# Storing the convolution branch as two halves, loading a merge's groups ahead, and transposing before scoring

## The chip, the cores and the metric

The kernel runs on one core of a Trainium2 chip. The metric is the device time of one execution in microseconds (us). Five engines matter: PE multiplies matrices, ACT (ScalarE), DVE (VectorE) and POOL (GpSimd) work elementwise, and SP issues nearly all DMA transfers. Each of them takes its instructions in the order in which the program lists them, and waits for other engines on semaphores.

## The reference

One layer for 1024 prompt tokens and 32 sample tokens, so T = 1056 columns, all in float32. Cut to what matters here:

```python
h, b_gate, c_gate, q, k, v, g_conv, g_att = split(xn @ w_in)
u = c_gate * h
y_conv = conv_w[0]*u[t-2] + conv_w[1]*u[t-1] + conv_w[2]*u[t]     # causal, 3 taps
conv_out = (b_gate * y_conv) @ w_conv_out
# for each of three dilation groups, 8 heads: softmax(q k / 8 + bias) v, with its log-sum-exp
wts = softmax(stack(lses), axis=0); o = sum(wts * stack(outs), axis=0)
attn_out = o @ w_attn_out
x = x + gate1 * ((sigmoid(g_conv) * conv_out + sigmoid(g_att) * attn_out) @ w_o)
x = x + gate2 * (relu(norm(x) @ w_mlp_in)**2 @ w_mlp_out)
```

## The kernel before

Activations lie with 128 features on the partitions and the 1056 columns along them. Every float32 operand of a large product is split in two: `hi`, a copy rounded to the matmul type fp32r, and `lo`, the remainder `x - hi`; three matmuls (hi·hi, hi·lo, lo·hi) make one product. A tile of 352 columns and 1024 features takes 24 matmuls (L377).

The program is written out by hand in one order. Long matmul jobs set the beat: after each half tile (or each bank of a paired job) `slot()` is called, and it emits other work in between: first what `later` holds for this slot (a list of functions with a countdown in slots), then attention work (`bg`, as far as a credit of `rate` per slot allows), then two paced lanes (`paced[0]`: the sample tokens' attention, `paced[1]`: the merges), whose generators say with `yield n` how many slots they pause.

The stages, with the times of the trace before:

- **Paired jobs** (about 130 to 430 us). Jobs H, C and B for two feature blocks at a time (`pair_job`, seven products n = 0 to 6, each for two column halves p = 0, 1, so 14 slots a job). Each product's bank is emptied by ACT or DVE: ACT copies n = 0 to `ps_s` (L269) and n = 2 to `ps_z` (L274). The p = 1 half uses one of two PSUM banks called `ps_s`, so the matmuls of n = 2, p = 1 can begin only when n = 0, p = 1 has been copied out. POOL forms sums of weights (`ws`, L229 to L232) and multiplies y, a page `yc` of 128x1056, by the gate in job B (L839); y is then stored to `yb_d` in DRAM (L846) during the next job. There are four such rounds, a store of two pages each.
- **Projections q, k, v with the prompt's attention between them** (about 540 to 1140 us). A visit of `attention` takes a pair of tiles: P·V of the pair before last, scores of this pair (L973, DVE adds the bias and takes the maximum in L979, ACT takes the exponent in L987), and transposes (L102) of the pair before, whose results DVE or ACT copy from banks `ps_pt` and `ps_g` to `S` (L99, L96). The decode lane and the sample values use the one bank `ps_pt` too.
- **Convolution output** (about 1140 to 1280 us): three chunks of 352 columns, eight tiles each. `conv_ops` loads the eight pages of a chunk from `yb_d` (`ybr`, L672) and splits them (`ybh` on ACT, `ybl` on DVE or POOL) in steps placed by `later`. The last attention visits, the decode lane's last group and merges run beside it.
- **Merges** (`merge`, one for each of four head pairs): weights of the three groups to DRAM (`w_d`), then for each group a broadcast load of its weights (`wb`, two DMAs) and its output (`og`), a product on DVE (L1252), a sum on POOL (L1257); at the end a split to `oh` and `ol` (L1263, L1265). All four must be done before the **attention output** (24 tiles of 12 matmuls, from about 1282 us), which reads them.
- Then w_o, and the channel mixer.

Of the kernel before, what the change touches and what calls it, by code (L numbers as in the profile page):

```python
# [9 lines left out]
F32 = mybir.dt.float32  # L10
F32R = mybir.dt.float32r
AF = mybir.ActivationFunctionType
ALU = mybir.AluOpType
# [9 lines left out]
KD = 8  # L23
# [26 lines left out]
class Trunk:  # L50
# [613 lines left out]

    def conv_ops(self, ch):
        nc = self.nc
        out, raws = [], {}

        def load(i):
            raw = raws[i] = self.page("ybr", (P, 3, CH))  # L670
            for x in range(3 if i < 2 else 2):
                nc.sync.dma_start(out=raw[:, x], in_=self.yb_d[3 * i + x][:, ch * CH:(ch + 1) * CH])  # L672

        def work(i):
            raw = raws.pop(i)
            h, l = self.page("ybh", (P, 3, CH), F32R), self.page("ybl", (P, 3, CH), F32R)
            for x in range(3 if i < 2 else 2):
                self.split(h[:, x], l[:, x], raw[:, x], CH, lo_on="pool" if x % 2 else "dve")
                out.append((h[:, x], l[:, x]))
            if i < 2:  # L680
                load(i + 1)
                self.later.append((2, lambda: work(i + 1)))
        load(0)
        self.later.append((2, lambda: work(0)))
        return out

    def qk_epilogue(self, is_k, g, j, c, ps, st):
# [138 lines left out]
    def conv_b(self, m):  # L826
        nc = self.nc

        def fin(mi, t, p, a, ps, op, last):
            if not last:  # L830
                b = self.chunk("ps_t")[:, :H]
            else:
                b = a
            c0 = (2 * p + t) * H
            nc.vector.tensor_tensor(out=b, in0=a, in1=ps, op=op)

            def mul():
                y = self.y[mi][:, c0:c0 + H]
                nc.gpsimd.tensor_tensor(out=y, in0=y, in1=b, op=ALU.mult)  # L839
            if last:  # L840
                mul()
            else:
                self.later.append((3, mul))

        def store(i):
            nc.sync.dma_start(out=self.yb_d[m + i], in_=self.y[i])  # L846
            self.y[i] = None
        for i in range(2):
            self.later.append((16 + i, lambda i=i: store(i)))
        return fin  # L850

    def keep_gate(self, i, g):
# [70 lines left out]
    def attention(self):  # L923
        st = {}
        p1 = p2 = None
        while True:
            pair = [self.items.popleft() for _ in range(2)] if self.items else None
            if pair is None and p1 is None and p2 is None:
                if self.done:
                    break  # L930
                yield None
                continue
            cost = 400
            if pair is not None and pair[0][2]:
                u = pair[0][0]
                if u["bias"] is None:
                    u["bias"] = self.load_bias(u["g"], u["j"])
                self.values(u)
                yield -1200
            for it in p2 or ():  # L940
                self.att_pv(it, st)
                cost += 120 * it[1][2]
            if pair is not None:
                self.att_scores(pair, st)
                cost += sum(450 + 130 * it[1][2] for it in pair)
            for it, n in zip(p1 or (), ("pt", "g")):
                self.att_tr(it, st, n)
                cost += 200 * it[1][2]
            yield -cost
            if p2 is not None and p2[1][3] and p2[1][0]["g"] == ORDER[2]:  # L950
                self.paced[1].append(self.merge(p2[1][0]["j"]))
            p1, p2 = pair, p1
# [270 lines left out]
    def merge(self, j):  # L1223
        nc = self.nc
        wk = self.chunk("wk", (P, 4, 2, 16))
        wk, M = wk[:, 0:3], wk[:, 3]
        for g in range(3):
            nc.sync.dma_start(out=M if g == 2 else wk[:, g], in_=self.st_d[g][j].rearrange("s h (b i) -> (h b) s i", i=16))
        yield 2
        nc.vector.tensor_copy(wk[:, 2].rearrange("p s (t y) -> p s t y", y=2), M.rearrange("p s (y t) -> p s t y", y=2))  # L1230
        mm, s = [wk[:, g, 0] for g in range(3)], [wk[:, g, 1] for g in range(3)]
        nc.vector.tensor_tensor(out=M[:, 0], in0=mm[0], in1=mm[1], op=ALU.max)
        nc.vector.tensor_tensor(out=M[:, 0], in0=M[:, 0], in1=mm[2], op=ALU.max)
        nc.vector.tensor_tensor(out=wk[:, :, 0], in0=wk[:, :, 0], in1=M[:, 0:1].to_broadcast([P, 3, 16]), op=ALU.subtract)
        nc.scalar.activation(wk[:, :, 0], wk[:, :, 0], AF.Exp)
        nc.vector.tensor_tensor(out=wk[:, :, 1], in0=wk[:, :, 0], in1=wk[:, :, 1], op=ALU.mult)
        nc.vector.tensor_tensor(out=M[:, 0], in0=s[0], in1=s[1], op=ALU.add)
        nc.vector.tensor_tensor(out=M[:, 0], in0=M[:, 0], in1=s[2], op=ALU.add)
        nc.vector.reciprocal(M[:, 1], M[:, 0])
        nc.vector.tensor_tensor(out=wk[:, :, 0], in0=wk[:, :, 0], in1=M[:, 1:2].to_broadcast([P, 3, 16]), op=ALU.mult)  # L1240
        yield 1
        nc.sync.dma_start(out=self.w_d[j].rearrange("g h (b i) -> (h b) g i", i=16), in_=wk[:, :, 0])
        del wk, M, mm, s
        yield 1
        acc = None
        for g in range(3):
            w, o = self.page("wb", (P, NP)), self.page("og", (P, NP))
            for hh in range(2):
                nc.sync.dma_start(out=w[64 * hh:64 * hh + 64], in_=self.w_d[j][g, hh].unsqueeze(0).to_broadcast([64, NP]))
            nc.sync.dma_start(out=o, in_=self.o_d[g][j])  # L1250
            yield 3
            nc.vector.tensor_tensor(out=o, in0=o, in1=w, op=ALU.mult)  # L1252
            del w
            if acc is None:
                acc = o
            else:
                nc.gpsimd.tensor_tensor(out=acc, in0=acc, in1=o, op=ALU.add)  # L1257
            del o
            yield 1
        yield 1  # L1260
        self.oh[j], self.ol[j] = self.page("oh", dt=F32R), self.page("ol", dt=F32R)
        yield 1
        nc.scalar.copy(self.oh[j][:, 0:NP], acc)  # L1263
        yield 1
        nc.vector.tensor_tensor(out=self.ol[j][:, 0:NP], in0=acc, in1=self.oh[j][:, 0:NP].bitcast(F32), op=ALU.subtract)  # L1265
        del acc
        yield 1
# [3 lines left out]
    def run(self):  # L1271
# [10 lines left out]
        self.o_d = [self.dp.tile([4, P, NP], F32, name=f"o_d{g}") for g in range(3)]  # L1282
        self.st_d = [self.dp.tile([4, 2, 2, NP], F32, name=f"st_d{g}") for g in range(3)]
        self.w_d = self.dp.tile([4, 3, 2, NP], F32, name="w_d")
        self.yb_d = self.dp.tile([KD, P, T], F32, name="yb_d")
        self.gate_d = self.dp.tile([16, P, T], F32, name="gate_d")

        w_in = t["w_in"]
# [53 lines left out]
        def begin(g, j, st):  # L1342
            self.sample_values(g, j, st["v"]["v"])
            self.add_unit(g, j, st["q"], st["k"], st["v"]["v"])
            if (g, j) == units[-1]:
                self.done = True
                self.rate = 1500.0
            else:
                self.rate = self.work / 18 * 0.85

# [607 lines left out]
```

## Time and profile before

| | |
|---|---|
| median of three executions | 2165.97 us (2165.32 to 2166.70) |
| the profiled execution | 2163.8 us, of which the traced span 2162.0 us |
| PE busy | 2021.7 us, 94% of the span |
| DVE, ACT, POOL busy | 65%, 46%, 36% |
| DMA | 325.84 MB, mean 151 GB/s |

Times in the rows are microseconds from the start of the span. A busy PE counts matmuls whose pipelined ends overlap. PEclk is the granted TensorE clock as a share of full speed.

### The profile page before, as it was taken

The numbers are of one execution on the slowest core, as the hardware profiler recorded it, in microseconds if no ns is written. First come the engines' busy times: TensorE is split into PE (matmuls) and PEld (weight loads), VectorE is DVE, ScalarE is ACT, GpSimd is POOL, SyncE is SP. The second block draws the span as 40 slices with busy tenths as digits, with TensorE's granted clock in tenths as the row PEclk, the third lists the DMA queues.
The fourth block names the chain that finished last, engine by engine and source line by source line (L and its number), as shares of the span: only waits on it lengthen the run. The fifth ranks groups of instructions, "written<-read, shape, count | busy, mean of one in ns | idle before, by whom it ended". The sixth has DMA issues, their size and how long they took to land.

```text
span 2162.0 us, 38832 instructions
## 1 busy us (share of the span) xinstructions
PE 2021.7 (94%) x15092; PEld 1907.2 (88%) x15092; DVE 1404.3 (65%) x2935; ACT 989.3 (46%) x2193; POOL 782.6 (36%) x553
## 2 busy tenths in 40 slices
PE   5899999999999999999997989988999999999998
PEld 2799999889899888888886878988999999999998
DVE  4846665435656666556676676378444447999997
ACT  4522223335566556555554322355555556433332
POOL 3645555320111111100011114235233235788785
PEclk8899999999999999999998999999999999999999
DMA  7242221764122445333246774432347729555542
GB/s 284 71 136 62 79 70 35 250 212 148 45 69 74 144 149 167 104 114 116 67 125 199 238 233 145 162 125 88 130 158 274 256 90 350 203 202 198 197 158 102
DMA packets 138096, 325.84 MB, mean 151 GB/s; under 512 B 34232, under 2 KB 77880, under 8 KB 136888
## 3 DMA queue, kind: packets, MB, share of 16 engines
q1 hardware_dynamic: 137480, 323.17, 44.5%
q8 instruction: 118, 1.93, 0.4%
q14 instruction: 66, 0.54, 0.1%
q10 hardware_dynamic: 432, 0.20, 0.0%
HBM read 270.48 MB, written 112.07 MB: 177 GB/s over the span
## 4 chain that ended last, share of the span: by engine, by line
PE 56%; DVE 23%; ACT 5%; issue 3%; DMA 3%; POOL 2%; SPq 0%; DVEq 0%; POOLq 0%; ACTq 0%
PE ps_g L377 23%; DVE acc L1721 5%; DVE wprod L162 5%; PE ps_g L264 4%; PE ps_s L264 4%; PE ps_g L266 4%; PE ps_s L266 4%; PE ps_s L265 4%; PE ps_g L265 4%; DVE hl L1573 1%; DVE wlo L197 1%; ACT S L987 1%; PE ps_o L1015 1%; DVE S L979 1%; PE ps_s L973 1%
## 5 line engine op out<-in xcount | busy, mean ns | idle before, releaser
L162 DVE TENSOR_TENSOR wprod<-wraw,wprod 128x512 fp32r<-128x512 f32 x276 | 270.1, 981 | 173.9 <-ACT wprod L158 173.8
L377 PE MATMUL ps_g<-xh,whi 128*128 128x352 f32 x1056 | 356.6, 338 | 12.8 <-ACT whi L193 6.5
L377 PE MATMUL ps_g<-xh,wlo 128*128 128x352 f32 x1056 | 346.3, 328 | 5.6 <-DVE wlo L197 5.4
L377 PE MATMUL ps_g<-xl,whi 128*128 128x352 f32 x1056 | 346.6, 328 | 3.0 <-POOL xl L406 2.2
L377 PEld LDWEIGHTS ps_g<-xh,whi 128*128 128x128 f32 x1056 | 203.2, 192 | 35.6 <-issue 16.1
L158 ACT CAST wprod<-wraw 128x512 fp32r<-128x512 f32 x276 | 163.3, 618 | 151.0 <-DVE wprod L162 104.1
L377 PEld LDWEIGHTS ps_g<-xl,whi 128*128 128x128 f32 x1056 | 203.9, 193 | 5.9 <-POOL xl L406 4.0
L377 PEld LDWEIGHTS ps_g<-xh,wlo 128*128 128x128 f32 x1056 | 202.7, 192 | 7.2 <-DVE wlo L197 7.2
L197 DVE TENSOR_TENSOR wlo<-wraw,whi 128x512 fp32r<-128x512 f32 x184 | 130.0, 748 | 45.6 <-PE ps_g L377 25.4
L162 POOL TENSOR_TENSOR lo<-qn,hi 128x1024 fp32r<-128x1024 f32 x12 | 33.2, 2770 | 346.7 <-ACT hi L158 346.7
L277 POOL TENSOR_TENSOR ps_z<-ps_z,ps_s 128x264 f32<-128x264 f32 x64 | 60.3, 944 | 252.0 <-DVE ps_s L276 251.8
L264 PE MATMUL ps_s<-th,wprod 128*128 128x264 f32 x512 | 146.3, 286 | 1.7 <-DVE ps_s L276 1.7
L264 PE MATMUL ps_g<-th,wprod 128*128 128x264 f32 x512 | 146.9, 287 | 0.0
L266 PE MATMUL ps_g<-th,wprod 128*128 128x264 f32 x512 | 145.8, 285 | 0.0
L265 PE MATMUL ps_s<-tl,wprod 128*128 128x264 f32 x512 | 145.8, 285 | 0.0
L266 PE MATMUL ps_s<-th,wprod 128*128 128x264 f32 x512 | 145.7, 285 | 0.0
L265 PE MATMUL ps_g<-tl,wprod 128*128 128x264 f32 x512 | 145.5, 284 | 0.0
L987 ACT ACTIVATE S<-S,ng 128x128 f32<-128x128 f32 (+1 forms) x192 | 84.2, 441 | 124.7 <-DVE ng L982 122.8
L193 ACT CAST whi<-wraw 128x512 fp32r<-128x512 f32 x184 | 104.2, 619 | 32.1 <-DMA wraw<-in_w_conv_out 11.4
L264 PE MATMUL ps_g<-xh,wprod 128*128 128x264 f32 x384 | 110.6, 288 | 3.2 <-ACT wprod L158 3.2
L266 PE MATMUL ps_g<-xh,wprod 128*128 128x264 f32 x384 | 110.3, 287 | 3.5 <-DVE wprod L162 3.5
L264 PE MATMUL ps_s<-xh,wprod 128*128 128x264 f32 x384 | 109.9, 286 | 3.4 <-DVE ps_s L280 3.4
(383 smaller groups left out, 6448.3 us busy)
## 6 DMA issues: line engine op xcount, KB each, us to landing
wraw<-in_w_in SPq DMA_DIRECT2D x76, 512.0 KB, 4.1
wada<-in_w_ada SPq DMA_DIRECT2D x48, 512.0 KB, 5.6
hid_d<-hid SPq DMA_DIRECT2D x32, 528.0 KB, 2.9
wraw<-in_w_mlp_in SPq DMA_DIRECT2D x32, 512.0 KB, 6.1
wraw<-in_w_mlp_out SPq DMA_DIRECT2D x32, 512.0 KB, 3.9
hraw<-hid_d SPq DMA_DIRECT2D x56, 264.0 KB, 4.4
kv<-in_v SPq DMA_DIRECT2D x28, 512.0 KB, 5.6
wraw<-in_w_conv_out SPq DMA_DIRECT2D x24, 512.0 KB, 6.7
```

What stands on the lines that cost most here:

```text
L158: nc.scalar.copy(hi, src)
L162: eng.tensor_tensor(out=lo, in0=src, in1=hi.bitcast(F32), op=ALU.subtract)
L193: self.nc.scalar.copy(hi[:, s], w[:, s])
L197: self.nc.vector.tensor_tensor(out=lo[:, s], in0=w[:, s], in1=hi[:, s].bitcast(F32), op=ALU.subtract)
L264: nc.tensor.matmul(ps, hi, xh, start=(k == 0), stop=False)
L265: nc.tensor.matmul(ps, hi, xl, start=False, stop=False)
L266: nc.tensor.matmul(ps, lo, xh, start=False, stop=(k == 3))
L277: nc.gpsimd.tensor_tensor(out=z[p], in0=z[p], in1=s[p], op=ALU.add)
L377: self.nc.tensor.matmul(ps, a, x, start=(i == 0), stop=(i == n - 1))
L973: nc.tensor.matmul(ps[hh][:, 256 * i:256 * i + N], q[a][pr, q0:q0 + P], k[b][pr, k0:k0 + N], start=(x == 0), stop=(x == 2))
L987: nc.scalar.activation(s, s, AF.Exp, bias=ng[:, hh, i:i + 1], accum_out=sm[:, hh, i:i + 1])
L1721: nc.vector.tensor_tensor(out=a, in0=a, in1=ps, op=ALU.add)
```

## The change

Three edits, and a number. (1) y is split where it is made: `later` places, for each of the two pages of a round, an ACT copy to a new page `yh` (`high`), a DVE subtraction in place (`low`), and two stores, to `ybh_d` and `ybl_d` (`store`). On SP's queue the two weight loads (L180) that stood behind the first store of a round stand ahead of all four. `conv_ops` only loads the halves, three pages a DMA. (2) `merge` has its loads in a function, and loads group g + 1 before it handles group g, with fewer pauses: 10 slots from the store of the weights to the copy `oh`, where there were 15. (3) In a visit the transposes come before the scores. The attention's `rate` behind the last unit is 2000 in place of 1500.

```diff
     def conv_ops(self, ch):
-        out, raws = [], {}
+        out = []
         def load(i):
-            raw = raws[i] = self.page("ybr", (P, 3, CH))
-            for x in range(3 if i < 2 else 2):
-                nc.sync.dma_start(out=raw[:, x], in_=self.yb_d[3 * i + x][:, ch * CH:(ch + 1) * CH])
-
-        def work(i):
-            raw = raws.pop(i)
-            h, l = self.page("ybh", (P, 3, CH), F32R), self.page("ybl", (P, 3, CH), F32R)
-            for x in range(3 if i < 2 else 2):
-                self.split(h[:, x], l[:, x], raw[:, x], CH, lo_on="pool" if x % 2 else "dve")
-                out.append((h[:, x], l[:, x]))
+            n = 3 if i < 2 else 2
+            h, l = self.page("ybh", (P, 3, CH)), self.page("ybl", (P, 3, CH))
+            for a, d in ((h, self.ybh_d), (l, self.ybl_d)):
+                nc.sync.dma_start(out=a[:, 0:n], in_=d[3 * i:3 * i + n, :, ch * CH:(ch + 1) * CH].rearrange("x p n -> p x n"))
+            for x in range(n):
+                out.append((h[:, x].bitcast(F32R), l[:, x].bitcast(F32R)))
             if i < 2:
-                load(i + 1)
-                self.later.append((2, lambda: work(i + 1)))
+                self.later.append((2, lambda: load(i + 1)))
         load(0)
-        self.later.append((2, lambda: work(0)))
...
     def conv_b(self, m):
+        def high(i):
+            h[i] = self.page("yh", dt=F32R)
+            nc.scalar.copy(h[i], self.y[i])
+        def low(i):
+            l[i] = self.y[i].bitcast(F32R)
+            nc.vector.tensor_tensor(out=l[i], in0=self.y[i], in1=h[i].bitcast(F32), op=ALU.subtract)
         def store(i):
-            nc.sync.dma_start(out=self.yb_d[m + i], in_=self.y[i])
+            nc.sync.dma_start(out=self.ybh_d[m + i], in_=h.pop(i).bitcast(F32))
+            nc.sync.dma_start(out=self.ybl_d[m + i], in_=self.y[i])
         for i in range(2):
-            self.later.append((16 + i, lambda i=i: store(i)))
+            for n, f in enumerate((high, low, store)):
+                self.later.append((15 + 3 * i + n, lambda i=i, f=f: f(i)))
...
     def attention(self):
+            for it, n in zip(p1 or (), ("pt", "g")):
+                self.att_tr(it, st, n)
             if pair is not None:
                 self.att_scores(pair, st)
-            for it, n in zip(p1 or (), ("pt", "g")):
-                self.att_tr(it, st, n)
...
     def merge(self, j):
+        wo = deque([load(0)])
+        yield 1
         acc = None
         for g in range(3):
-            yield 3
+            if g < 2:
+                wo.append(load(g + 1))
+            yield 2
+            w, o = wo.popleft()
             nc.vector.tensor_tensor(out=o, in0=o, in1=w, op=ALU.mult)
...
-            yield 1
-        yield 1
+        yield 2
         self.oh[j], self.ol[j] = self.page("oh", dt=F32R), self.page("ol", dt=F32R)
-        yield 1
...
-                self.rate = 1500.0
+                self.rate = 2000.0
```

How the first round of the paired jobs stands on ACT, from the last weight cast before job H on (`yc_1420` is the first page y, `yh` its half; brackets name the semaphores waited for), before:

```order
L158 CAST wprod_1677<-ws1_1634 128x512 [waits PE_49,Pool_49]
L269 COPY ps_s_1693<-ps_g_1680 128x264 [waits PE_49]
L269 COPY ps_s_1708<-ps_s_1695 128x264 [waits PE_49]
L158 CAST wprod_1715<-wraw_1438 128x512 [waits DVE_49,Pool_49]
L158 CAST wprod_1747<-wraw_1440 128x512 [waits DMAHW6_49]
L274 COPY ps_z_1763<-ps_g_1750 128x264 [waits PE_49]
```

And with the change:

```order
L158 CAST wprod_1678<-ws1_1635 128x512 [waits PE_49,Pool_49]
L269 COPY ps_s_1694<-ps_g_1681 128x264 [waits PE_49]
L843 CAST yh_1696<-yc_1420 128x1056 [waits Pool_49]
L269 COPY ps_s_1711<-ps_s_1698 128x264 [waits PE_49]
L158 CAST wprod_1718<-wraw_1439 128x512 [waits DVE_49]
L843 CAST yh_1751<-yc_1501 128x1056 [waits DMAHW3_49,DVE_49]
L158 CAST wprod_1753<-wraw_1441 128x512 [waits DMAHW6_49]
L274 COPY ps_z_1769<-ps_g_1756 128x264 [waits PE_49]
```

The first new copy, which waits for POOL, stands between the two copies that empty n = 0; the second, which waits for a DMA (the store of the first `yh`, whose buffer it takes again), stands before the copies that empty n = 2.

How ACT stands in the convolution output's first tiles, from the copy of the transposed values `vt` on (L987 and, in the changed file, L994 are the exponents of a visit, L96 copies transposed S out of PSUM), before:

```order
L96 COPY vt<-ps_g 128x512
L987 ACTIVATE S,st<-S,ng 128x128 x2
L987 ACTIVATE S,st<-S,ng 128x256 x2
L96 COPY S<-ps_g 128x512
L193 CAST whi<-wraw 128x512 x2
L158 CAST ybh<-ybr 128x352 x3
L987 ACTIVATE S,st<-S,ng 128x256 x4
L96 COPY S<-ps_pt 128x256
L193 CAST whi<-wraw 128x512 x2
L158 CAST ybh<-ybr 128x352 x3
L987 ACTIVATE S,st<-S,ng 128x256 x4
L96 COPY S<-ps_pt 128x512
```

And with the change:

```order
L96 COPY vt<-ps_g 128x512
L96 COPY S<-ps_g 128x512
L994 ACTIVATE S,st<-S,ng 128x128 x2
L994 ACTIVATE S,st<-S,ng 128x256 x2
L193 CAST whi<-wraw 128x512 x2
L96 COPY S<-ps_pt 128x256
L994 ACTIVATE S,st<-S,ng 128x256 x4
L96 COPY S<-ps_pt 128x512
L994 ACTIVATE S,st<-S,ng 128x256 x4
L193 CAST whi<-wraw 128x512 x2
```

The copies that free the transposes' banks stand ahead of the visit's exponents instead of behind them, the casts of `ybr` are gone, and two visits follow each other without weight casts between.

How SP's queue stands around the third merge's loads, from the store of its weights on (`sg` is one gate load for each tile), before:

```order
L1242 DMA w_d<-wk 128x3x16
L1385 DMA sg<-gate_d 128x352
L672 DMA ybr<-yb_d 128x352 x3
L1249 DMA wb<-w_d 64x1024 x2
L1250 DMA og<-o_d_85 128x1024
L180 DMA wraw<-in_w_conv_out 128x1024
L672 DMA ybr<-yb_d 128x352 x3
L1385 DMA sg<-gate_d 128x352
L1084 DMA kv<-in_k1T 128x2x512 x2
```

And with the change:

```order
L1249 DMA w_d<-wk 128x3x16
L1398 DMA sg<-gate_d 128x352
L1255 DMA wb<-w_d 64x1024 x2
L1256 DMA og<-o_d_85 128x1024
L180 DMA wraw<-in_w_conv_out 128x1024
L1255 DMA wb<-w_d 64x1024 x2
L1256 DMA og<-o_d_86 128x1024
L1398 DMA sg<-gate_d 128x352
L180 DMA wraw<-in_w_conv_out 128x1024
L1255 DMA wb<-w_d 64x1024 x2
L1256 DMA og<-o_d_87 128x1024
```

Two groups are now asked for within one gate load, all three within two; the chunk's pages are asked for behind them.

## Rows read from the trace of the kernel before

**Rows 1.** Busy time by stage: us, engines busy, PEclk, DMA share, GB/s.

```profile
108.00:432.00 324.00, 317.05 (x2561) 308.56 (x2560) 189.37 (x371) 96.35 (x195) 168.06 (x163) 1.00 0.33 105
540.00:1140.00 600.00, 573.59 (x4291) 516.35 (x4291) 378.99 (x1040) 343.25 (x880) 71.33 (x34) 0.99 0.33 106
1140.00:1294.00 154.00, 128.66 (x962) 118.61 (x960) 104.69 (x261) 55.66 (x137) 22.16 (x15) 0.93 0.74 228
```

**Rows 2.** What PE waited for, 1140 to 1294 us: total, times, longest.

```profile
PE ps_pt L1070 <- ACT S L96: 7.8, 1, 7.8
PE ps_s L1143 <- DMA kv<-in_k1T: 4.5, 2, 3.6
PE ps_pt L102 <- DVE S L99: 4.3, 1, 4.3
PE ps_g L377 <- DVE wlo L197: 3.2, 2, 2.4
PE ps_pt L102 <- DVE wk L1230: 2.3, 1, 2.3
PE ps_o L1015 <- ACT S L96: 1.4, 1, 1.4
```

**Rows 3.** PE's timeline at the attention output: start, duration, [idle before <-releaser].

```profile
1301.64 0.66 PE L377 MATMUL ps_g<-oh,whi 128*128 128x352 f32 x1 [9.34 <-ACT oh L1263]
...
1303.66 0.49 PE L377 MATMUL ps_g<-oh,whi 128*128 128x352 f32 x1
1303.95 0.49 PE L377 MATMUL ps_g<-ol,whi 128*128 128x352 f32 x1
...
1307.90 0.32 PE L377 MATMUL ps_g<-oh,whi 128*128 128x352 f32 x1
1308.06 0.32 PE L377 MATMUL ps_g<-ol,whi 128*128 128x352 f32 x1
```

**Rows 4.** ACT's timeline at the longest wait of rows 2.

```profile
1178.75 0.51 ACT L987 ACTIVATE S<-S,ng 128x256 f32<-128x256 f32 x1 [5.89 <-DVE ng L982]
...
1180.73 0.56 ACT L96 COPY S<-ps_pt 128x512 f32<-128x512 f32 x1
```

**Rows 5.** What PE waited for, 540 to 1140 us.

```profile
PE ps_pt L1074 <- ACT S L96: 3.4, 1, 3.4
PE ps_pt L102 <- ACT S L96: 3.3, 2, 2.6
```

**Rows 6.** Instructions on tile ybr, 1100 to 1300 us: duration ns min/median/max.

```profile
L158 ACT CAST ybh<-ybr x24: 470/484/488, 1124.3 to 1236.1; 128x352 fp32r<-128x352 f32 x24
L162 DVE TENSOR_TENSOR ybl<-ybr,ybh x15: 511/526/2475, 1126.0 to 1235.9; 128x352 fp32r<-128x352 f32 x15
L162 POOL TENSOR_TENSOR ybl<-ybr,ybh x9: 930/948/1639, 1125.2 to 1236.7; 128x352 fp32r<-128x352 f32 x9
```

**Rows 7.** DMA with nothing left over: one stretch by engine.

```profile
1150.00:1162.00 12.00, 12.00 (x84) 11.40 (x84) 7.15 (x18) 5.42 (x16) 0.00 (x0) 0.83 1.01 293
```

**Rows 8.** POOL's timeline, first round: the last two products of the first y.

```profile
184.81 1.93 POOL L839 TENSOR_TENSOR yc<-yc,ps_z 128x264 f32<-128x264 f32 x2
```

**Rows 9.** ACT's timeline, first round: the copy that frees n = 0, p = 1.

```profile
181.25 0.38 ACT L269 COPY ps_s<-ps_s 128x264 f32<-128x264 f32 x1
```

**Rows 10.** PE's timeline, first round: where n = 2, p = 1 begins.

```profile
183.72 0.28 PE L264 MATMUL ps_s<-th,wprod 128*128 128x264 f32 x1
```

**Rows 11.** The stores of y (source line L846): first and last start, landing.

```profile
L846 SPq DMA_DIRECT2D yb_d<-yc x8: 326/384/487, 186.8 to 378.6; - x8
...
DMA to landing us min/median/max: 6.8/7.4/8.2
```

**Rows 12.** SP's timeline, first round: what follows the first store.

```profile
187.21 1.28 SPq L180 DMA_DIRECT2D wraw<-in_w_in x2
```

**Rows 13.** Stores of the same size elsewhere, from the page: KB, us to landing.

```profile
hid_d<-hid SPq DMA_DIRECT2D x32, 528.0 KB, 2.9
```

**Rows 14.** An ACT copy of 128x1056 to fp32r: count, busy, mean ns.

```profile
L1565 ACT CAST hh<-hraw 128x1056 fp32r<-128x1056 f32 x49 | 52.8, 1078 | 33.3 <-POOL hraw L1577 32.6 <-DVE hraw L1577 0.5 <-DMA hraw<-hid_d 0.2
```

More of the change, by code (lines that the diff above doesn't have):

```diff
@@ L843, in fin @@
                 self.later.append((3, mul))
+        h, l = {}, {}
+        def high(i):
[4 more added lines that the diff above has]
+            nc.vector.tensor_tensor(out=l[i], in0=self.y[i], in1=h[i].bitcast(F32), op=ALU.subtract)
         def store(i):
-            nc.sync.dma_start(out=self.yb_d[m + i], in_=self.y[i])
+            nc.sync.dma_start(out=self.ybh_d[m + i], in_=h.pop(i).bitcast(F32))
+            nc.sync.dma_start(out=self.ybl_d[m + i], in_=self.y[i])
+            l.pop(i)
             self.y[i] = None
         for i in range(2):
-            self.later.append((16 + i, lambda i=i: store(i)))
+            for n, f in enumerate((high, low, store)):
+                self.later.append((15 + 3 * i + n, lambda i=i, f=f: f(i)))
         return fin
@@ L942, in attention @@
                 cost += 120 * it[1][2]
+            for it, n in zip(p1 or (), ("pt", "g")):
+                self.att_tr(it, st, n)
+                cost += 200 * it[1][2]
             if pair is not None:
@@ L945, in attention @@
                 cost += sum(450 + 130 * it[1][2] for it in pair)
-            for it, n in zip(p1 or (), ("pt", "g")):
-                self.att_tr(it, st, n)
-                cost += 200 * it[1][2]
             yield -cost
@@ L1244, in merge, with load @@
         yield 1
-        acc = None
-        for g in range(3):
+        def load(g):
             w, o = self.page("wb", (P, NP)), self.page("og", (P, NP))
@@ L1250, in merge @@
             nc.sync.dma_start(out=o, in_=self.o_d[g][j])
-            yield 3
+            return w, o
+        wo = deque([load(0)])
+        yield 1
+        acc = None
+        for g in range(3):
+            if g < 2:
+                wo.append(load(g + 1))
+            yield 2
+            w, o = wo.popleft()
             nc.vector.tensor_tensor(out=o, in0=o, in1=w, op=ALU.mult)
@@ L1284, in run @@
         self.w_d = self.dp.tile([4, 3, 2, NP], F32, name="w_d")
-        self.yb_d = self.dp.tile([KD, P, T], F32, name="yb_d")
+        self.ybh_d, self.ybl_d = (self.dp.tile([KD, P, T], F32, name=n) for n in ("ybh_d", "ybl_d"))
         self.gate_d = self.dp.tile([16, P, T], F32, name="gate_d")
```

## The prediction

> **What bounds the kernel now.** I read the page's shares first: PE is busy for 94% of the span. So a gain or a loss counts only where it fills or opens an idle time of PE. I then cut the span into the stages that the change touches [rows 1]. In the paired jobs and in the attention PE is busy for 98% and 96% of the time, at a clock of 1.00 and 0.99. In the convolution output, from 1140 to 1294 us, it is 84%, the clock is 0.93, and the DMA share more than doubles, to 0.74. I next took PE's waits in that last stage [rows 2]: the long ones are on `S`, the copies of transposed scores, 7.8 + 4.3 + 1.4 = 13.5 us. The next view, ACT's timeline at the longest of them, shows why: the copy is behind exponents that themselves waited 5.89 us for a maximum from DVE [rows 4]. Right after the stage stands one wait of 9.3 us, on the copy `oh` of the last merge [rows 3].
>
> **Removed: the transposes' wait.** With the change the copies of `S` are issued ahead of the visit's exponents. From 1178.75 us, where the first exponent starts, to 1180.73, where the copy starts, is 1.98 us; and the first exponent's own wait was 5.89 [rows 4]. Neither stands ahead of the copy any more. The splits of `ybr`, which share these queues, go as well: 24 casts of 484 ns on ACT, 15 subtractions of 526 ns on DVE, whose longest took 2475 ns, and 9 on POOL [rows 6]. I credit the three waits whole: -13.5 us.
>
> **Removed: the wait for the last merge.** The merge takes 10 slots instead of 15. Attention finishes some 3 slots earlier as its visits stand closer and the paced lanes go on meanwhile. Eight slots are eight half tiles, far over the 9.3 us [rows 3]: the last merge ends beside the convolution's tiles. -9.3 us.
>
> **Removed: the slow clock after a wait.** After the wait for `oh` matmuls start 0.29 us apart, and later 0.16 [rows 3]: that is the 1.2 GHz level and the 2.4 GHz level. The slow pace lasts from 1301.64 to some point between 1303.95 and 1307.90. At the middle, 4.3 us at 0.29 hold matmuls that need 4.3 x 0.16 / 0.29 = 2.4, so 1.9 us are lost. For the two long waits on `S` I take 1.5 each, as their idle times are shorter. -4.9 us.
>
> **Removed: smaller waits.** In the steady attention the same copies cost 3.4 + 3.3 = 6.7 us [rows 5]; ACT has other work ahead of them there, so I credit half, -3.4. In the last stage `wlo` (3.2) and `wk` (2.3) wait for DVE [rows 2], which loses its splits: -5.5. The sample keys' wait of 4.5 us [rows 2] is a DMA's and stays. At the least these bring nothing: nothing shows that DVE would be earlier at just those places.
>
> **Added in the convolution output.** Each chunk now reads both halves of eight pages, 24 more reads of 128x352 floats, 180 KB each: 4.33 MB. At the 293 GB/s of a stretch in which the engines are full [rows 7] this is 14.8 us. Over 154 us with a share of 0.74 [rows 1] 40 us are free, so most of it is hidden; in the full stretches [rows 7] it would not be. Between 0 and 14.8 us I take 4, nearer the free share. The two visits that now follow each other directly find a chain of exponents in their way: 0 to 5 us, by the 5.89 of [rows 4]; I take 1.5.
>
> **Added in the paired jobs: a wait on POOL.** This is the part that speaks against the change. The new ACT copy of the first page y waits for POOL's last product on it, which ends at 184.81 + 1.93 = 186.74 us [rows 8]; that SP's store of the page started at 186.8 [rows 11] agrees. But in ACT's queue this copy stands ahead of the copy that frees n = 0, p = 1. Before, that copy was at 181.25 [rows 9], and PE began n = 2, p = 1 at 183.72 [rows 10]. Now it starts after 186.74 + 1.08 for the new cast [rows 14], takes 0.38 [rows 9], and ends at 188.2: PE stands for 188.2 - 183.7 = 4.5 us, plus 1.5 of slow clock. PE has no other work in its queue there, since it was 98% busy [rows 1]; the wait is not hidden. Four rounds of the same form make 4 x 6 = 24 us. It could be 0 if POOL ended its products early, as it would if they did not wait for PE's banks; and at most 4 x (4.5 + 1.9) = 25.6, with the slow clock lasting as long as after the wait for `oh`.
>
> **Added in the paired jobs: a wait on a store.** The second new copy takes the buffer of the first `yh` again in rounds 1 to 3, so ACT waits there for the landing of that page's store, issued at about 188 us. ACT's following casts of weights and the copies that empty n = 2 stand behind it. PE needs these some three slots after 188.2; the four rounds' stores lie some 63 us apart [rows 11], a round is three jobs of 14 slots, so a slot is 1.5 us and the need is at about 192.7. Two rows bound the landing: 2.9 us for stores of this size elsewhere [rows 13], and 7.4 for the stores of y in this very place [rows 11]. There two weight loads are issued 0.4 us behind the first store [rows 12] and share the engines with it. With the change these loads stand ahead of the stores on SP's queue, and are no longer held by the store that waited for POOL; they run early, and the store meets only the other stores. So I take the value near 2.9: 0.5 us a round, 1.5 in all. At 7.4 ACT goes on at 188 + 7.4 = 195.4, and PE stands about 3 us longer, with 1.5 of slow clock: some 4.6 a round, 13.8 in all. It decides from a landing of about 4.7 us.
> The Trainium skill, "DMA: Bandwidth & Descriptors", section "Anatomy of one DMA — SWDGE (gpsimd) path", gives about 2.0 us and a microsecond per 436 KB for a DMA that GpSimd issues, which would be an estimate of 3.2 us for 541 KB; SP's queue is another path. By that rule the second wait costs next to nothing; the 2.9 us agree with it, the 7.4 don't.
> DVE's subtraction in place, eight of them, and eight more stores, 4.3 MB, find DVE at 189 of 324 us and the DMA share at 0.33 [rows 1]: nothing, unless DVE stands behind ACT for long.
>
> **The sum.** Removed: 13.5 + 9.3 + 4.9 + 3.4 + 5.5 = 36.6. Added: 4 + 1.5 + 24 + 1.5 = 31.0. Net -5.6 us. The profiled execution took 2163.8 us, 1.8 of them around the span; it becomes 2158.2. The median of the runs is 2.2 above it: 2160.4, so 2160 us.
>
> **The rivals.** First, slower: the store's landing decides. If the second copy waits for 7.4 us [rows 11], the rounds cost 13.8 instead of 1.5: +12.3, 2172.7 us. For it: it is the same store in the same place. Against it: the weight loads that disturbed it are now ahead.
> Second, no change: the waits that only a faster DVE or ACT could shorten stay. Without the 3.4 and 5.5 the sum is +3.3: 2169.3 us. For it: `wlo` and `wk` end on DVE, whose queue also holds merges that are now crowded together. Against it: DVE loses 15 subtractions.
> Third, the halves' reads eat the gain: 14.8 us instead of 4, 2171.2 us, at the bound between no change and slower. For it: the engines are full in [rows 7]. Against it: 40 us are free in the stage.
> Fourth, the rounds cost nothing in the first wait, because PE's banks or POOL's products turn out in another order than I read: 24 less, 2136 us. For it: POOL's spans are rough. Against it: the store at 186.8, which waited for the same product [rows 11].
>
> **How the numbers follow.** I give the forecast 0.45, the first rival 0.18, the second 0.12, the third 0.10, the fourth 0.13, and 0.02 to the rest. A difference of 0.2%, 4.3 us, is about what a measurement of this kernel can tell from no change; so faster is below 2161.6 and slower above 2170.3. The forecast lies only 1.6 us inside faster; with some 8 us of spread around 2160 I divide its 0.45 into 0.30 faster, 0.13 the same, 0.02 slower. With the fourth rival faster is 0.44, with a little of the rest; the second and 0.03 of the third make the same 0.28; the first, 0.07 of the third and the rest make slower 0.28. The range reaches from the fourth rival at 2136 to 2180, some way above the first, short of the first and third together (2183.5). The likeliest case alone spans 2152 to 2168.
>
> **What would show it.** In the paired jobs PE must wait for ACT's `ps_s` copy four times, about 4.5 us each and 63 us apart, with a granted clock below 1.00 there, and ACT must wait for POOL on `yc` just before. A landing of the first `yh` store under 5 us speaks for the forecast, over 5 for the first rival. In the convolution output PE's waits on `S` must shrink to a few microseconds, the wait for `oh` must be gone, and the DMA share must be above 0.74 with the stage shorter than 154 us. The prediction is wrong if PE stays at 98% in the paired jobs, or if the tail keeps over half of its 13.5 + 9.3 us.

## The result, and the profile of the changed kernel

The changed kernel takes 2190.15 us (median of four executions, 2187.55 to 2192.57) against 2165.7 us before: ratio 1.011, 95% interval 1.0094 to 1.0126. It is slower by 24 us, where 6 us less were forecast, and outside the range.

I cut both traces at the same places of PE's work: start and end of the convolution output, start and end of the attention output. Before, the two stages are these (columns as in [rows 1]: the stretch and its length, the busy time of PE, of its weight loads, of DVE, ACT and POOL, then PEclk, DMA share and GB/s). The convolution output ends, and the attention output begins, at 1290.6 us, later than the 1280 and 1282 named above.

```profile
1141.60:1290.60 149.00, 125.36 (x935) 115.82 (x934) 100.42 (x253) 53.86 (x133) 19.79 (x14) 0.93 0.74 229
1290.60:1349.60 59.00, 49.06 (x288) 48.40 (x287) 37.95 (x62) 16.51 (x35) 26.85 (x24) 0.91 0.53 165
```

With the change, the paired jobs' window of [rows 1] and the same two stages:

```profile
108.00:432.00 324.00, 301.26 (x2372) 294.77 (x2371) 184.03 (x361) 96.31 (x186) 157.10 (x157) 0.97 0.30 101
1163.90:1327.30 163.40, 134.42 (x934) 120.87 (x933) 96.15 (x236) 47.35 (x119) 16.53 (x9) 0.90 0.74 233
1327.30:1373.70 46.40, 46.40 (x289) 46.40 (x288) 34.72 (x59) 13.85 (x28) 22.13 (x22) 1.00 0.55 182
```

The convolution output starts 22.3 us later, lasts 14.4 longer, the attention output 12.6 shorter, and the rest (812.4 and 812.0 us) is the same: 22.3 + 14.4 - 12.6 - 0.4 = 23.7, the difference of the spans. PE does the same matmuls in the middle stage (935 and 934 in the traces), but is busy for 9 us more at a lower clock and idle for 29.0 us instead of 23.6.

The first 22 us are the paired jobs. ACT's timeline of the first round answers to [rows 8 to 10]:

```profile
186.95 1.07 ACT L843 CAST yh<-yc 128x1056 fp32r<-128x1056 f32 x1 [4.92 <-POOL yc L833]
187.93 0.37 ACT L269 COPY ps_s<-ps_s 128x264 f32<-128x264 f32 x1
190.77 1.08 ACT L843 CAST yh<-yc 128x1056 fp32r<-128x1056 f32 x1 [1.95 <-DMA ybh_d<-yh]
```

and PE's waits from 108 to 432 us, and the landing of the eight stores of `yh` (us, min, median, max):

```profile
PE ps_s L264 <- ACT ps_s L269: 15.1, 4, 3.8
```

```profile
DMA to landing us min/median/max: 2.6/2.6/2.6
```

ACT stands 4.92 us for POOL and PE 3.8 us behind it, once in each of four rounds. The second copy's 1.95 us wait for the store costs PE next to nothing: PE waits 2.4 us for ACT's weight casts in the whole stretch, where it waited 1.7 before. The waits end at 188.35 us in the first and 395.61 in the fourth: 69.1 us a round instead of 63.4.

In the convolution output PE now waits for other things than in [rows 2]:

```profile
PE ps_g L377 <- DVE wlo L197: 7.8, 3, 4.5
PE ps_s L1150 <- DMA kv<-in_k1T: 7.1, 3, 5.2
PE ps_pt L102 <- DVE so L1217: 5.8, 1, 5.8
PE ps_g L377 <- ACT whi L193: 3.3, 2, 1.9
PE ps_pt L1081 <- DVE S L99: 2.9, 1, 2.9
PE ps_pt L102 <- ACT S L994: 1.6, 1, 1.6
PE ps_o L1022 <- DVE S L99: 0.2, 1, 0.2
```

The 13.5 us for copies of S have become 4.7; the weights' halves, the sample keys and `so` (the sample tokens' result on its way to a transpose) have grown by more. DVE's timeline at the first of these waits (PE stands 4.5 us for `wlo`) shows what is ahead of it:

```profile
1168.99 1.23 DVE L1267 TENSOR_TENSOR og<-og,wb 128x1024 f32<-128x1024 f32 x1 [2.42 <-DMA og<-o_d]
...
1172.70 0.53 DVE L1415 TENSOR_TENSOR mc<-ps_g,sg 128x352 f32<-128x352 f32 x1 [2.49 <-DMA sg<-gate_d]
1173.15 2.49 DVE L197 TENSOR_TENSOR wlo<-wraw,whi 128x512 fp32r<-128x512 f32 x4
```

DVE stands in order for a merge's group, then for a gate, whose loads were asked for one behind the other; `wlo`, whose weights are there, comes behind both. A second pattern is at the end of the stage, DVE and POOL side by side:

```profile
1288.05 1.28 DVE L197 TENSOR_TENSOR wlo<-wraw,whi 128x512 fp32r<-128x512 f32 x2
...
1293.40 3.31 DVE L197 TENSOR_TENSOR wlo<-wraw,whi 128x512 fp32r<-128x512 f32 x2
```

```profile
1293.18 2.38 POOL L1272 TENSOR_TENSOR og<-og 128x1024 f32<-128x1024 f32 x1 [36.68 <-PE ps_pt L102]
```

The two subtractions take 3.31 us while POOL sums a merge; elsewhere two take 1.28. The Trainium skill, "SBUF — State Buffer", section "Who interferes with whom", says that a DVE instruction with two SBUF inputs contends with a GpSimd instruction that reads SBUF, and calls the contention an exclusive lock; the 2 us more beside a sum of 2.38 us agree.

### The profile page after: what moved, and what is told of

The parts are those of the page before. It is cut to its first block, busy times and chain, and to the rows that moved or that the text cites. A ratio compares the mean times of both kernels' runs of the same rounds, so it can differ in the third digit from the quotient of the medians.

```text
span 2185.7 us, 38826 instructions
## 1 busy us (share of the span) xinstructions
PE 2039.8 (93%) x15092; PEld 1916.6 (88%) x15092; DVE 1397.5 (64%) x2928; ACT 989.3 (45%) x2177; POOL 768.9 (35%) x544
## 4 chain that ended last, share of the span: by engine, by line
PE 51%; DVE 19%; ACT 5%; DMA 3%; issue 2%; POOL 1%; SPq 1%; DVEq 0%; POOLq 0%; ACTq 0%
PE ps_g L377 24%; DVE acc L1734 5%; DVE wprod L162 4%; PE ps_g L264 3%; PE ps_s L264 3%; PE ps_s L265 3%; PE ps_s L266 3%; PE ps_g L266 3%; PE ps_g L265 3%; DVE wlo L197 1%; PE ps_s L980 1%; DVE hl L1586 1%; PE ps_o L1022 1%; ACT S L994 1%; PE ps_pt L102 1%
## 5 line engine op out<-in xcount | busy, mean ns | idle before, releaser
L377 PE MATMUL ps_g<-xh,whi 128*128 128x352 f32 x1056 | 356.6, 338 | 12.7 <-ACT whi L193 6.4
L264 PE MATMUL ps_s<-th,wprod 128*128 128x264 f32 x512 | 148.5, 290 | 16.8 <-ACT ps_s L269 15.1
L994 ACT ACTIVATE S<-S,ng 128x128 f32<-128x128 f32 (+1 forms) x192 | 84.2, 440 | 103.5 <-DVE ng L989 103.5
L264 PEld LDWEIGHTS ps_s<-th,wprod 128*128 128x128 f32 x512 | 98.2, 192 | 18.5 <-ACT ps_s L269 16.0
```

What stands on the lines that cost most here:

```text
L264: nc.tensor.matmul(ps, hi, xh, start=(k == 0), stop=False)
L377: self.nc.tensor.matmul(ps, a, x, start=(i == 0), stop=(i == n - 1))
L994: nc.scalar.activation(s, s, AF.Exp, bias=ng[:, hh, i:i + 1], accum_out=sm[:, hh, i:i + 1])
```

## The experiments

Each job ran the kernel before beside its kernels; its medians were 2162.9 to 2165.25 us. Stage lengths are from the traces, cut as above: before, convolution output 149, attention output 59, together 208 us. A bracket behind a ratio is its 95% interval.

**The three edits alone.** Each is its hunks of the diff above and nothing else; the rate stays 1500.

```diff
 e1: + high, low, store; conv_ops loads halves
 e2: + wo = deque([load(0)]) ... wo.append(load(g + 1)) ... yield 2
 e3: + att_tr before att_scores
```

> The kernel before with edit 1 alone (y split where it is made, the halves stored and loaded). Common to all theories: the paired jobs cost what they cost in the changed kernel, four steps of about 5.7 us, +23. Theory A (the halves' 4.3 MB more of reads crowd the DMA engines, so weights, gates and sample keys come late): the convolution output is longer than before by 8 us or more, 2195 us or above. Theory B (the merges' loads, asked for two groups at once, crowd out gates and weights, and DVE stands in order behind their products): the convolution output is no longer than before, since ACT and DVE lose the splits, 2181 to 2189 us.

> The kernel before with edit 2 alone (a merge's groups loaded ahead, fewer pauses). Both: the wait of 9.3 us for the last merge goes, 12 us with its slow clock. Theory A (the halves' reads): nothing else changes, 2151 to 2156 us. Theory B (the merges' bursts): the convolution output becomes some 10 us longer, 2160 to 2168 us.

> The kernel before with edit 3 alone (transposes ahead of the scores, rate 1500 as before). Both theories A and B: PE's three waits on S in the convolution output, 13.5 us, shrink to under 5 us and nothing comes in their place, 2150 to 2158 us. Theory C (those waits are places where PE would have waited for something else anyway, a DMA or DVE): within 4 us of before.

Edit 1: 2185.56 us, ratio 1.0103 (1.0087 to 1.0119); convolution output 147.9. The halves' reads, with the splits gone, don't lengthen that stage (A is out, the loss is the rounds'). Edit 2: 2162.61, ratio 0.9998 (0.9985 to 1.0011); attention output 46.1, convolution output 165.6: what one stage gains the other loses (the stages before them are 4.4 us shorter). Edit 3: 2163.18, ratio 0.9999 (0.9989 to 1.0009): theory C, nothing. Its waits in the convolution output:

```profile
PE ps_g L377 <- DVE wlo L197: 3.6, 3, 1.8
PE ps_s L1143 <- DMA kv<-in_k1T: 3.6, 2, 3.0
PE ps_pt L1074 <- DVE dS L1071: 3.1, 1, 3.1
PE ps_pt L102 <- DVE S L99: 2.8, 1, 2.8
...
PE ps_pt L1070 <- ACT S L96: 1.3, 1, 1.3
```

Those on S fell from 13.5 to 4.1 us, but the stage only from 149.0 to 146.0: the next operands on DVE and DMA were late by almost as much. The three runs together account for 22 of the 24 us; no run changes the rate alone.

**The copies five slots later**, behind those that empty n = 0 and n = 2.

```diff
-                self.later.append((15 + 3 * i + n, lambda i=i, f=f: f(i)))
+                self.later.append((20 + 3 * i + n, lambda i=i, f=f: f(i)))
```

> The changed kernel with the two ACT copies, the subtractions and the stores of the halves five slots later, so that the first copy stands behind the copies that empty n = 0 and n = 2. All theories: ACT no longer waits for POOL in front of them, the four waits of 3.8 us and their slow clock go, the paired jobs take 63.4 us a round again, and the time is 2190 - 23 = 2167 us (2163 to 2170). If the rounds stay at 69 us, the wait is not ACT's order but something else.

2167.46 us, 1.0026 (1.0016 to 1.0037), as expected. PE's wait for `ps_s` on ACT is gone from 108 to 432 us; ACT's four waits for POOL, 19.6 us, are now

```profile
  POOL yc L833: 3.0, 3
```

The convolution output begins at 1143.8 us instead of 1163.9, so 20 of the rounds' 22 us come back. It is still 163.3 us long, so the rounds and this stage are two separate losses.

**Which part of edit 2 costs.** e5: the short pauses, each group loaded after the one before. e6: edit 2 for the last merge. e7: edit 2 with its loads, of the weights `wb` too, issued by POOL. e8: the changed kernel, later copies, without edit 2. The main lines:

```diff
 e5, against the kernel before:
-            yield 3
+            yield 2
...
-        yield 1
...
-        yield 1
 e6, against the kernel before:
...
+        ahead = j == 3
...
 e7, against e2:
...
-            nc.sync.dma_start(out=o, in_=self.o_d[g][j])
+            nc.gpsimd.dma_start(out=o, in_=self.o_d[g][j])
```

> The kernel before with a merge's pauses cut to the same 10 slots as in edit 2, but each group loaded only after the group before it was handled. Theory B (edit 2 alone gained nothing because the loads of two groups at once push back gates and weights): without the burst the attention output keeps its 46 us, the convolution output falls back from 166 to 153 us or less, 2148 to 2157 us. Theory D (the two stages are bound by all their transfers and by DVE together, and a wait taken away in one comes back in the other): convolution output and attention output together stay at 208 us, give or take 4, and the time within 4 us of before.

> The kernel before with edit 2 for the last merge only (j = 3); the other three as before. Theory B: the burst of the last merge meets the end of the convolution output, where few loads are left, so the 12 us of the wait for oh are gained and at most 4 given back, 2150 to 2157 us. Theory D: within 4 us of before, the convolution output 160 us or longer.

> The kernel before with edit 2 alone, but the merges' loads (wb, og) issued by POOL on a queue of its own instead of SP's. Theory B in the form that the order on SP's queue decides (gates and weights stand behind wb and og, and behind SP's wait for the weights w_d to land): gates land in 4 us or less instead of 6 to 9, convolution output 153 us or less, 2148 to 2157 us. Theory D, or B in the form that the DMA engines are full: the convolution output stays at 160 us or more, 2159 us or more.

> The changed kernel with the halves' copies five slots later (as in the run before) and without edit 2. Theory B: the convolution output falls from 163 to 150 us or less, the wait for oh comes back (59 us), 2160 to 2166 us. Theory A (halves' reads crowd the DMA): the convolution output stays over 155 us and the time is 2170 us or more.

e5: 2156.34, 0.9969 (0.9958 to 0.9981); the time is in B's range, but the stage is 160.6 us without any burst where B named 153, so B's reason fails here; D had the two stages together right (206.0), but not the time, since the stages before were 3 us shorter. e6: 2160.67, 0.9988 (0.9977 to 0.9999); the wait for `oh` is still 5.9 us, since this merge starts as late as before, and the convolution output is 150.0: too little gained for B, too short a stage for D. e7: 2177.1, 1.007 (1.0049 to 1.0091), stage 175.8, far beyond what the other side's 2159 named: gates do land sooner (a median of 3.9 us instead of 7.0 in e2), so their order on SP's queue is not what makes this stage long; on a queue of its own `og` lands after a median of 13.7 us instead of 8.5, and PE's wait for `wlo` grows from 10.7 to 23.8 us. e8: 2162.6, 0.9997 (0.9983 to 1.0011), 147.3 and 58.9 as B said. The next view was what DVE waited for in the stage. In e2 and e7:

```profile
DVE og L1260 <- DMA og<-o_d: 9.9, 4, 4.7
```

```profile
DVE og L1260 <- DMA og<-o_d: 29.7, 5, 10.3
```

Before it is 3.7 us, in e8 4.2, in the changed kernel 10.7, in e5 19.0. The four kernels with a short merge have the long waits and the long stages, though e5 waits more than e2 in a shorter stage. From that came theory E.

**Products on POOL (e9 to e11), and a longer pause (e12).** The lines are against e2 (e9, e12), the run with the later copies (e10), and edits 2 and 3 together (e11).

```diff
 e9, e10, e11:
-            nc.vector.tensor_tensor(out=o, in0=o, in1=w, op=ALU.mult)
+            nc.gpsimd.tensor_tensor(out=o, in0=o, in1=w, op=ALU.mult)
 e12:
         wo = deque([load(0)])
-        yield 1
+        yield 3
```

> The kernel before with edit 2 alone, but the merges' products og = og x wb made by POOL instead of DVE. Theory E (with shorter pauses DVE reaches the product before og has landed, stands there in order, and the weight halves wlo and the transposes' copies behind it come late for PE: DVE waited 3.7 us for og before, 9.9 with edit 2 alone, 19.0 in the short merge, 29.7 with the merge's own queue): PE's wait on wlo falls from 10.7 to 4 us or less, the convolution output from 166 to 153 us or less, the attention output stays at 46, 2146 to 2154 us. Theory D (the two stages are bound by all their transfers together): they stay at 206 us or more, 2158 us or more.

> The changed kernel with the halves' copies five slots later and the merges' products on POOL. Theory E: DVE's wait for og (10.7 us) goes, the convolution output falls from 163 to 153 us or less, 2150 to 2158 us. Theory D: as with the later copies alone, 2164 us or more.

> The kernel before with edits 2 and 3 (no stored halves) and the merges' products on POOL. Theory E: the waits on S and for og both go, convolution and attention output together take 196 us or less, 2144 to 2152 us. Theory D: 2158 us or more.

> The kernel before with edit 2 alone, but three slots instead of one behind the first load, so that the first product comes five slots after its load. Theory E: DVE's wait for og falls to 4 us or less, PE's wait on wlo to 5 us or less, convolution output 155 us or less, 2149 to 2157 us. Theory D: 2159 us or more.

e9: 2169.97, 1.0029 (1.0016 to 1.0041). e10: 2169.84, 1.003 (1.002 to 1.004). e11: 2171.16, 1.0035 (1.0024 to 1.0047). All three against E and as D expected: DVE no longer waits for `og`, and the stage is 170.9, 163.5 and 172.4 us; in e9 PE waits 13.5 us for `wlo`. The stage of e9, for comparison with e2's 105.36 us of DVE and 24.46 of POOL:

```profile
1144.70:1315.60 170.90, 131.11 (x937) 119.75 (x936) 107.44 (x244) 56.83 (x140) 47.88 (x25) 0.88 0.67 208
```

DVE has nine products of 1.2 us less and is still busy for 2 us more, beside a POOL with twice the work: its other instructions became longer by some 13 us, nearly all of it in the 48 subtractions `wlo` (762 ns each in e2, 1025 in e9). So taking the products off DVE takes away one wait and feeds the other pattern. e12: 2150.87, 0.9948 (0.9929 to 0.9968), DVE waits no time for `og`, stages 152.3 and 46.1. That is against D, and meets E in three of its four numbers, but not in the one that E's path runs through: PE's wait on `wlo` is 11.9 us, not 5 or less. What went is the wait for `so` (7.1 us in e2, 0.6) and for `whi` (4.2, 0.9).

**Shift or burst.** e13: the changed kernel with later copies and e12's pause. e14: edit 2 with `yield 3` in place of `yield 1` between the store of `w_d` and the first load. e15: e5 with products on POOL. e16: e12 with edit 3.

```diff
 e14:
         del wk, M, mm, s
-        yield 1
+        yield 3
```

> The changed kernel with the halves' copies five slots later and two slots more behind a merge's first load. If the cause of the long convolution output is the same there as with edit 2 alone (B or F), it falls from 163 to 153 us or less and the time from 2167 to 2152 to 2158 us. If the gain of the longer pause was a matter of one lucky place (G), it needn't hold here: 2162 us or more.

> The kernel before with edit 2 alone, but three slots instead of one between the store of w_d and the first load; the second group's load still one slot behind the first. Theory F (SP waits up to 3.4 us for w_d to land, all loads behind it come late and together): SP's wait goes, 2148 to 2156 us. Theory B (the burst of two groups): the burst is the same, convolution output 160 us or more, 2158 us or more.

> The short merge (10 slots, each group loaded only after the one before) with the products on POOL: no burst, and DVE doesn't stand for og (19.0 us in the short merge). Theory B: convolution output 153 us or less, 2156 us or less. Theory G or D: as the short merge or slower, 2156 us or more, with a convolution output over 158 us.

> The kernel before with edits 2 and 3 and two slots more behind a merge's first load. All theories in which the waits on S are independent of the merges: a little below the longer pause alone, 2144 to 2151 us. Theory G (places collide by chance): anywhere up to 2163 us.

e13: 2151.3, 0.9938 (0.9916 to 0.9961), stage 146.6. e14: 2148.07, 0.9916 (0.9895 to 0.9936). e15: 2161.85, 0.9983 (0.9971 to 0.9995), stage 163.2. e16: 2148.19, 0.992 (0.9903 to 0.9936), stage 145.8. In e13 and e16 the two slots help as in e12, so G's lucky place is not needed; a shift by another number of slots was not run. e14 keeps the burst and is, with e16, the fastest; e5 and e15 have none and long stages: the burst by itself is not the cause. Nor is it the pause between a load and its product, which is the same in e14 as in e2 (three slots for the first group, four for the others; three for each before). SP's wait for `w_d` in e14 is 5.7 us against 6.6 in e2, so F, which expected it to go, has the time right but not the reason. The stages of e14:

```profile
1141.50:1291.00 149.50, 126.18 (x937) 116.87 (x936) 104.73 (x250) 56.04 (x140) 25.08 (x16) 0.92 0.77 238
1291.00:1336.70 45.70, 45.70 (x286) 45.70 (x285) 36.42 (x59) 13.84 (x28) 22.50 (x22) 1.00 0.56 183
```

DVE's timeline shows where two slots matter. In e2, merge 2 and then the end of the stage:

```profile
1213.04 1.23 DVE L1260 TENSOR_TENSOR og<-og,wb 128x1024 f32<-128x1024 f32 x1 [4.69 <-DMA og<-o_d]
1220.45 1.23 DVE L1260 TENSOR_TENSOR og<-og,wb 128x1024 f32<-128x1024 f32 x1 [3.75 <-DMA og<-o_d]
...
1274.86 3.17 DVE L197 TENSOR_TENSOR wlo<-wraw,whi 128x512 fp32r<-128x512 f32 x2
1280.42 0.20 DVE L1210 COPY so<-so 128x64 f32<-128x64 f32 x1
```

What ends PE's two long waits there is a load each time, not a product: weights that were asked for among the merge's groups, and pages `ybr` asked for behind them (PE's waits, then ACT's).

```profile
1224.40 0.43 PE L377 MATMUL ps_g<-ybh,whi 128*128 128x352 f32 x1 [4.19 <-ACT whi L193]
1232.50 0.66 PE L377 MATMUL ps_g<-ybh,wlo 128*128 128x352 f32 x1 [7.51 <-DVE wlo L197]
```

```profile
1223.73 1.14 ACT L193 CAST whi<-wraw 128x512 fp32r<-128x512 f32 x2 [7.83 <-DMA wraw<-in_w_conv_out]
1229.49 1.47 ACT L158 CAST ybh<-ybr 128x352 fp32r<-128x352 f32 x3 [4.61 <-DMA ybr<-yb_d]
```

In e14 the products of merge 2 find their group landed, and the last `so` is done just before the last merge's first product:

```profile
1228.61 1.21 DVE L1260 TENSOR_TENSOR og<-og,wb 128x1024 f32<-128x1024 f32 x1
...
1269.81 0.20 DVE L1210 COPY so<-so 128x64 f32<-128x64 f32 x1
1269.91 1.22 DVE L1260 TENSOR_TENSOR og<-og,wb 128x1024 f32<-128x1024 f32 x1
```

PE's idle times over 0.6 us in the stage sum to 36.1 us in e2 and 23.3 in e14: 11.7 against 7.3 at the weights of the tiles near 1220 us, and 8.7 against 1.5 after 1265 us. Before, they sum to 23.6, with 0.8 at those weights and 4.6 at the end of the stage.

**The last merge alone, and the whole change.** e17: e2 with `yield 3 if j == 3 else 1` at e14's place. e18: the changed kernel with the later copies and e14's line.

> The kernel before with edit 2 alone, the last merge (j = 3) two slots later, the other three as in edit 2. Theory H (the last merge's DVE products and POOL sums lie among the sample tokens' last steps; there edit 2 alone lost 8.7 us in three waits, 1.3 + 1.6 + 5.8, and the shifted burst 1.5): these waits fall to 3 us or less, the convolution output from 166 to 159 us or less, 2152 to 2157 us. Theory I (the loss lies at tiles 10 to 12, where weights come late behind the second merge's loads; 11.7 against 7.3 us): convolution output 161 us or more, 2158 us or more.

> The changed kernel with the halves' copies five slots later and every merge two slots later (three in place of one between the store of w_d and the first load). Theory H: convolution output 153 us or less, 2147 to 2155 us. If the collision comes back in another place: 2160 us or more.

e17: 2157.65, 0.9975 (0.9964 to 0.9986), stages 162.9 and 45.8: H fails by the length of the stage and I holds (its time lies between theirs), for the loss at merge 2 stays, and the sample tokens' steps, late from it, still meet the last merge (PE's waits, then DVE's):

```profile
PE ps_pt L102 <- DVE so L1210: 7.6, 1, 7.6
```

```profile
DVE og L1260 <- DMA og<-o_d: 11.1, 4, 4.7
```

e18: 2149.32, 0.9943 (0.993 to 0.9956), stages 142.7 and 46.0, inside H's range, though e17 had already spoken against H's reason. One large wait is left:

```profile
PE ps_s L1150 <- DMA kv<-in_k1T: 13.0, 4, 11.2
```

PE's wait on the sample keys is 6.0 to 14.2 us in each of the seven kernels with edit 1 and 4.5 or less in the thirteen without it. What holds the keys back there was not tested.

So with its copies five slots and its merges two slots later the whole change beats the kernel before by 0.6%; edit 2 with the shift alone (e14) by 0.8%. The two intervals overlap, so no gain of edit 1 is shown.

## Why the prediction was wrong

- **Wait on POOL: right.** 4.5 us a round and 24 in all were forecast; 3.8 a round, 15.1 in all; a round is 5.7 longer with the slow clock, 22.8 in all. e4 gave 20 of them back.
- **Wait on the first halves' store: right.** It lands in 2.6 us (2.9 taken, 7.4 the other end), so the first rival fell; the fourth fell with the wait on POOL, which came.
- **Wait for the last merge: right in its own stage.** -9.3 and -1.9 were forecast, -12.6 measured. PE also stood 0.6 us for `ol`, and in the trace before the slow pace lasted to 1307.5 us, not to the middle of the two rows.
- **Halves' reads: right to be small.** 4 us taken; in e1 the stage is 1 us shorter than before, with the splits gone. The third rival fell; the longer wait on the sample keys is not explained.
- **"The last merge ends beside the convolution's tiles": the step that failed.** I costed it at nothing and named no work that hides it. Edit 2 alone made that stage 16.6 us longer. PE is idle there for 12.7 us more than before and busy for 3.9 more. The merges run earlier, and their instructions and loads meet others: weights and pages asked for beside merge 2's groups come late (11.7 us, where it was 0.8), and the last merge's products and sums lie among the sample tokens' last steps (8.7 where it was 4.6). In the changed kernel DVE also stands for `og` in front of `wlo` (the wait of 4.5 us). I counted only the slots saved, and not where the merges' work would lie.
- **The transposes' wait, credited whole (-13.5): wrong in size.** The waits did shrink by 9 us, but e3 gained 3 us in the stage and nothing in the time. The -3.4 of the steady attention is not seen either: in e3 those waits fall from 6.7 to 1.4 us, but the convolution output starts 2 us later than before.
- **Smaller waits (-5.5) and the clock (-3.0 of the 4.9): wrong in sign.** `wlo` went from 3.2 to 7.8, `whi` from none to 3.3; PE is busy for 9.1 us more on the same instructions.

For the stage I had -13.5 - 3.0 - 5.5 + 4 + 1.5 = -16.5; it became +14.4. These 31 us are the whole miss (30 us, from -5.6 to +24.4). 16.6 of them are edit 2's; 12.4 are edits 1 and 3, forecast at -16.5 together, which alone made -1.1 and -3.0; the last 2 appear only with all edits together. That the rest of the sum came out within 2 us is in part luck: the rounds cost 2.7 us less than forecast, and the -3.4 did not come. Two of the signs named beforehand failed in this stage: the DMA share stayed at 0.74, and the stage is 163.4 us, not shorter than 154. The second rival, in which the smaller waits stay, pointed this way but priced it at 9 us.

Still open: how the 16.6 us divide between loads that land late beside a merge's groups, DVE standing for `og`, POOL's sums stretching DVE's subtractions, and the clock. In e12 and e14 DVE no longer stands for `og`, yet PE still waits 8.8 and 7.3 us for weights at merge 2, behind pages `ybr` that land late. No run stopped the stretching alone; that it comes from POOL is read from the timelines and from the 48 subtractions in e9. That a shift by two slots takes most of the loss away is shown by five kernels (e12, e13, e14, e16, e18); why two slots do it is argued from the timelines.

## What to carry to other kernels

A wait of the bottleneck engine is worth only the distance to the next late operand: before crediting it, look for what else would be late at the same place. When background work is moved forward, count where its instructions stand in each in-order queue, whether their loads have landed by then, and what other loads are asked for beside them; two slots took 13 and 16 us off one stage here (e12, e14). And a new instruction that waits for a slow engine belongs behind the copies that empty the matmul banks: five slots decided 20 us.

## What the runs showed of the hardware

DVE subtractions of 128x512 from SBUF slowed from 0.64 to about 1.6 us each while POOL summed in SBUF. In the changed kernel the eight stores of `yh`, 528 KB each, landed in 2.6 us, with the weight loads 10 us or more ahead of a round's first store; before, a store of y took a median of 7.4 us, with two weight loads issued between the two stores of a round, 0.4 us behind the first [rows 11, 12]. Loads of `og` issued by POOL landed after a median of 13.7 us (e7), by SP after 8.5 (e2), though POOL's queue held nothing but the merges' loads. In the convolution output PE was idle for 29.0 instead of 23.6 us and busy for 9 us more on the same matmuls, at a granted clock of 0.90 instead of 0.93.
